# A fourth slab buffer, and the sums of weights in four pieces, in the gate and up stage of an encoder block

## The chip, the core and the metric

The kernel runs on one core of one Trainium2 chip. The metric is the time of one execution on the device in microseconds (us), the median of several runs. A core has a matrix engine (TensorE; PE in the profile, and PEld for its weight loads), three engines for elementwise work (VectorE or DVE, ScalarE or ACT, GpSimd or POOL), a queue engine (SyncE or SP) that issues most transfers here, and 16 DMA engines. Each engine has its own list of instructions and works it off in order; between engines, semaphores order them.

## What is computed

One encoder block on a sequence of 256 rows of width 2048: four mixers side by side, cross attention to a memory of 256 rows, and a gated feed forward part. Only the last bears on the change:

```
def swiglu(h, w_gate_up, w_down):
    gate, up = jnp.split(h @ w_gate_up, 2, axis=-1)
    return (jax.nn.silu(gate) * up) @ w_down
...
    x = x + swiglu(rms_norm(x, norm_g[l, 2]), w_gate_up[l], w_down[l])
```

`w_gate_up` is 2048 x 11264 and `w_down` 5632 x 2048, all in fp32.

## The kernel before

**Weights as one stream.** All weight matrices are cut into blocks of 128 x 128, in the order in which PE wants them. 16 blocks are a slab (128 x 2048, 1 MB in HBM, the rows `W[n]`), and there are 252 slabs. The class `Stream` loads and prepares them. One `dma_start` on SP's queue brings a slab into a tile `raw` (line 96), of which there are three (`rawp`, line 229). A slab is then split by halves of eight blocks: ACT rounds the half to the reduced format (`wh`, line 120), DVE forms what is left over (`wl`, line 121). A product is three matmuls: rounded left by rounded weight (line 421), by the leftover of the weight (422), and leftover of the left side by rounded weight (423). `wh` and `wl` have three buffers each (`wp`, line 230), and `look` (line 158) issues the split of a half when PE's work on the half two before is about to be issued. So a half's cast can begin when PE has left the half three before.

**Gate and up** (`gate_up`, line 855). The 11264 columns are taken in 11 groups `j` of 2 x 512 (512 of gate and the matching 512 of up). A group goes over the 16 row blocks of the contraction in eight slabs `i`, each with two of them (`2i` and `2i + 1`). An ordinary slab has four pieces of 128 x 512, each used by two halves of the rows: 8 x 3 = 24 matmuls of 128 x 512. The results of a group stay in four PSUM banks `cs`; odd groups have the banks `pm`, even groups `pg`.

**Summed slabs.** In each group but the first, the slabs `i` = 1 and 5 (`SEVEN`, line 47) are done as a 2 x 2 block product with seven products in place of eight, on sums of blocks of the left side and of the weight. That is 7 x 3 = 21 matmuls (`unit`, line 883). Of the slab's four pieces of 512 columns, three are used as they are (unsummed) and four sums are used: two differences to the first piece, and two further ones built on those. `Stream._forms` (line 125) makes them all when the slab's turn comes in `_half`: ACT rounds the unsummed 1536 columns (`hb`, line 134), DVE makes the sums `t` (lines 135 to 138), ACT rounds them (`ht`, lines 136 and 139), DVE forms the leftovers of the unsummed (`lb`, line 140) and of the sums (`lt`, line 142). These tiles have one buffer each. Lines 135, 138, 140 and 142 go through a helper, and the profile puts all of them at line 133: there the tiles' names `t`, `lb` and `lt` tell them apart. There are 20 such slabs. Their products go to four more PSUM banks (`ps`), which are those that the group before has left.

**What else DVE and ACT do there.** After slab 5 of a group `combine` (line 894) merges the four banks of the summed products: four operations on DVE (`m`, `h`, `g`, `h`), one copy on ACT (line 899). After slab 7 `finish` (line 908) adds two banks each for gate and up (four DVE operations at line 248), applies silu on ACT (line 915, `g<-g,rc`), multiplies (line 252, `h<-h,rc,g`), and turns the result (line 450, `u<-h`), which POOL's queue then stores (line 453, `hidden<-u`). `fetch` (line 839) reads the hidden rows of the first groups back while gate and up still runs and splits them (lines 256 and 248, `act<-tmp` and `f<-tmp`), and `turn` (line 972) turns the residual (line 979). The last two end before the middle of the stage.

**What sets the order.** This side work is written as generators in a list. `Background` (line 178) steps them between products: each step is due after some PE time, and only while the DVE work that is counted as owed (`dve`, line 196; it falls as PE's time goes on) is under 0.9 us. `drain` issues the rest of a generator at once: `finish` is drained when slab 1 of the next group comes. What is issued is then ordered by engine when the program is laid out: an instruction may be set before one that was issued earlier. `keep_place` (line 274) forbids that for chosen instructions: it ties each to the one issued before it on its engine.

The two lines that say when a split is issued, and how many halves ahead (`extra` is None in this stage):

```
ahead = self.n // 8 + 1 + min(3 if self.extra else 2, self.n // 16)
while len(self.halves) < min(ahead, NBLK // 8):
```

Of the kernel before, what the change touches and what calls it, by code (L numbers as in the profile page):

```python
# [13 lines left out]
F32 = mybir.dt.float32  # L14
F32R = mybir.dt.float32r
# [3 lines left out]
ALU = mybir.AluOpType  # L19
# [3 lines left out]
P = 128  # L23
# [11 lines left out]
CUTS = {0: [0, 256, 512, 1024, 2048]}  # L35
# [14 lines left out]
def seven(slab):  # L50

    j, i = divmod(slab - GU // 16, 8)
    return 1 <= j < DFF // 512 and i in SEVEN
# [22 lines left out]
class Stream:  # L76


    def __init__(self, tc, pools, W, bg):
        self.tc, self.nc, self.W, self.bg = tc, tc.nc, W, bg  # L80
        self.rawp, self.wp = pools
        self.order = []
        self.n = 0
        self.after = []
        self.halves = []
        self.raw = None
        self.extra = None
        self.places = []

    def _half(self):  # L90

        nc, n = self.nc, 8 * len(self.halves)
        if n % 16 == 0:
            self.raw = self.rawp.tile([P, 2048], F32, name="raw", tag="raw")
            for a, b in zip(CUTS[n], CUTS[n][1:]) if n in CUTS else [(0, 1024), (1024, 2048)] if self.after else [(0, 2048)]:
                (nc.scalar if (n, a) == (0, 0) else nc.sync).dma_start(self.raw[:, a:b], self.W[n // 16][:, a:b])
                if self.after:
                    self.after.pop(0)()
        if seven(n // 16):
            self.halves += [self._forms(self.raw), None]  # L100
            return
        o = (n % 16) * P
        r = self.raw[:, o:o + 1024]
# [12 lines left out]
        at = 48 if any(a <= n < b for a, b in ROWS) else 8  # L116
        wh, wl = wh[:, at:at + 1024], wl[:, at:at + 1024]
        edges = [0, 256, 512, 1024] if n == 0 else [0, 512, 1024] if n == 8 else [0, 1024]
        for a, b in zip(edges, edges[1:]):
            nc.scalar.copy(wh[:, a:b], r[:, a:b])  # L120
            nc.vector.tensor_tensor(out=wl[:, a:b], in0=r[:, a:b], in1=wh[:, a:b].bitcast(F32), op=ALU.subtract)  # L121
        self.bg.dve(1024)
        self.halves.append((wh, wl))

    def _forms(self, raw):


        nc = self.nc
        hb, lb, ht, lt = (self.swp.tile([P, w], F32R, name=t, tag=t)
                          for t, w in (("hb", 1536), ("lb", 1536), ("ht", 2048), ("lt", 2048)))  # L130
        t = self.swp.tile([P, 2048], F32, name="t", tag="t")
        blk = raw.rearrange("p (b c) -> p b c", b=4)
        sub = lambda out, a, b: nc.vector.tensor_tensor(out=out, in0=a, in1=b, op=ALU.subtract)  # L133
        nc.scalar.copy(hb, raw[:, 512:2048])  # L134
        sub(t[:, 0:1024].rearrange("p (b c) -> p b c", b=2), blk[:, 1:4:2, :], blk[:, 0:1, :].to_broadcast([P, 2, 512]))
        nc.scalar.copy(ht[:, 0:1024], t[:, 0:1024])
        nc.vector.tensor_tensor(out=t[:, 1024:1536], in0=raw[:, 1536:2048], in1=t[:, 0:512], op=ALU.add)
        sub(t[:, 1536:2048], raw[:, 1024:1536], t[:, 1024:1536])
        nc.scalar.copy(ht[:, 1024:2048], t[:, 1024:2048])
        sub(lb, raw[:, 512:2048], hb.bitcast(F32))  # L140
        for a in (0, 1024):
            sub(lt[:, a:a + 1024], t[:, a:a + 1024], ht[:, a:a + 1024].bitcast(F32))
        self.bg.dve(5632, 6)
        cut = lambda x, y: [(x[:, a:a + 512], y[:, a:a + 512]) for a in range(0, x.shape[1], 512)]
        return cut(hb, lb) + cut(ht, lt)

    def take_forms(self, w, ks, c0, c1):

        assert self.n % 16 == 0 and seven(self.n // 16)
        self.look()  # L150
        forms = self.halves[self.n // 8]
        for k, c in ((ks[0], c1), (ks[0], c0), (ks[1], c0), (ks[1], c1)):
            self.order += [(w, k, c + i * P) for i in range(4)]
        self.n += 16
        self.halves[self.n // 8 - 2] = None
        return forms

    def look(self):
        ahead = self.n // 8 + 1 + min(3 if self.extra else 2, self.n // 16)
# [60 lines left out]
class Block:  # L220
    def __init__(self, ctx, tc, t):
        self.ctx, self.tc, self.nc, self.t = ctx, tc, tc.nc, t
        pool = lambda n, b, **kw: ctx.enter_context(tc.tile_pool(name=n, bufs=b, **kw))
        self.cp = pool("cp", 1)
        self.tp = pool("tp", 11)
        self.rp = pool("rp", 3)
        self.psG = pool("psG", 4, space=PSUM)
        self.psM = pool("psM", 4, space=PSUM)
        rawp = pool("rawp", 3)
        wp = pool("wp", 3)  # L230
        self.bg = Background()
        self.st = Stream(tc, (rawp, wp), t["W"], self.bg)
        self.kept = itertools.count()
        self.run()

# [588 lines left out]
    def mlp(self):  # L824
        tc, nc, act = self.tc, self.nc, self.act
        with tc.tile_pool(name="fp", bufs=1) as fp:
            self.gap(fp, 192)
            f = act[4:12] + [fp.tile([P, 512], F32R, name=f"f{i}") for i in range(EARLY - 8)]
            with tc.tile_pool(name="sw", bufs=1) as sw, tc.tile_pool(name="gp", bufs=1) as gp:
                self.st.swp = sw  # L830
                self.gate_up(sw, gp, f)
            with tc.tile_pool(name="hp", bufs=1) as hp:
                held = [hp.tile([P, 512], F32R, name=f"held{i}") for i in range(HELD // 2)]
                self.st.places = list(zip(held[0::2], held[1::2]))
                f += [hp.tile([P, 512], F32R, name=f"g{i}") for i in range(FT - 16 - EARLY)] + self.h3
                self.bg.add(self.fetch(f, EARLY, FT, 6, SOON))
                self.down(f)
# [17 lines left out]
    def gate_up(self, sw, gp, f):  # L855

        nc, st = self.nc, self.st
# [24 lines left out]

        def unit(i, cs, ps, start, stop, c0, c1):

            b11, b21, b22, u1, t3, t2, t4 = st.take_forms("w_gate_up", (2 * i, 2 * i + 1), c0, c1)
            whole = lambda k, r: [self.h3[k][:, a + r * P:a + (r + 1) * P] for a in (0, R)]
            formed = lambda n: [x[:, n * P:(n + 1) * P] for x in sums[i]]
            for p, a, b, own in ((ps[0], whole(2 * i, 0), b11, True), (cs[0][0], whole(2 * i + 1, 0), b21, False),
                                 (cs[0][1], formed(3), b22, False), (ps[1], formed(0), u1, True), (ps[2], formed(2), t3, True),
                                 (ps[3], formed(1), t2, True), (cs[1][0], whole(2 * i + 1, 1), t4, False)):  # L890
                self.part(p, *a, *b, own and start, own and stop)
                self.bg.poll()

# [38 lines left out]
        forms = self.bg.add(left())  # L932
        turned = self.bg.add(self.turn())
        early = end = None
        for j in range(DFF // 512):
            cols = [j * 512, DFF + j * 512]
            banks = [self.gbank, self.bank]
            cs = [[banks[j % 2]() for _ in cols] for _ in range(2)]
# [4 lines left out]
            for i in range(8):  # L943
# [700 lines left out]
```

## Time and profile before

| | |
|---|---|
| median of 3 runs | 1485.53 us (1484.07, 1485.53, 1493.59) |
| the profiled execution | 1481.33 us, of which the span of instructions is 1479.6 us |
| granted TensorE clock | 0.998 of full speed |
| gate and up, groups 1 to 10 | from about 802 to 1222 us of the span |
| down, to the end | from about 1222 us |

How to read the profile: an engine's busy time is the union of its instructions. The ends of matmuls are modelled and a matmul's bar reaches over the start of the next, so that a stream of matmuls without gaps looks like PE busy all the time; the pace is read from start to start, or from the count of weight loads, of which there is one a matmul. "Idle before" is the time in which an engine stood idle ahead of an instruction, and after the arrow stands what ended it. A transfer's landing is counted from its issue.

### The profile page before, as it was taken

Reading aid. Unit: us, or ns where it says so; the run is one execution under the profiler, and the core shown is the slowest. Engines: PE = TensorE matmul, PEld = TensorE weight load, DVE = VectorE, ACT = ScalarE, POOL = GpSimd, SP = SyncE. Lnnn points to the kernel's source line nnn. Section 1 sums busy time; section 2 is a strip of 40 time slices with the busy share of each in tenths; the row PEclk is TensorE's granted clock in tenths of the full one; section 3 lists DMA queues with packets and bytes.
Section 4 is the critical chain, followed back from the end, with each engine's and each line's share of the span. In section 5 each row is a group of like instructions: output and inputs, shape, how many; then the busy total and the mean of one; then the engine's idle time right before and its main releaser. Section 6 shows DMA issues by size and latency. Waiting matters only on the chain.

```text
span 1479.6 us, 19468 instructions
## 1 busy us (share of the span) xinstructions
PE 1459.8 (99%) x7296; PEld 1230.8 (83%) x7296; DVE 1066.3 (72%) x1548; ACT 793.3 (54%) x1172; POOL 161.4 (11%) x276
## 2 busy tenths in 40 slices
PE   9999999999999999999999999999999999999997
PEld 7878888898898888888888787778888888888886
DVE  6688668778777767877776877878877776644445
ACT  6565655467555556766554454554454544534344
POOL 0220100000000001200024311111101112000000
PEclk9999999999999999999999999999999999999999
DMA  9975554454535555544557757656665675655554
GB/s 357 337 260 210 197 200 170 148 181 164 201 129 206 182 200 199 189 167 168 180 183 248 244 202 252 214 198 228 225 228 198 213 241 192 239 188 196 199 198 144
DMA packets 56718, 306.09 MB, mean 207 GB/s; under 512 B 9485, under 2 KB 11182, under 8 KB 25008
## 3 DMA queue, kind: packets, MB, share of 16 engines
q1 hardware_dynamic: 45920, 281.11, 53.5%
q0 software_dynamic: 10272, 23.09, 5.4%
q8 instruction: 57, 0.93, 0.2%
q10 hardware_dynamic: 432, 0.66, 0.1%
q14 instruction: 37, 0.30, 0.1%
HBM read 291.18 MB, written 13.63 MB: 206 GB/s over the span
## 4 chain that ended last, share of the span: by engine, by line
PE 75%; DVE 12%; DMA 8%; issue 3%; ACT 2%; SPq 0%; DVEq 0%; ACTq 0%
PE pg L370 18%; PE pg L422 11%; PE pg L423 11%; PE pg L421 11%; PE pg L371 10%; DMA raw<-in_W 8%; DVE wl L121 5%; PE pm L423 2%; PE pm L422 2%; PE pm L421 2%; DVE t L133 2%; DVE lt L133 2%; DVE lb L133 1%; PE pm L1145 1%; ACT wh L120 1%
## 5 line engine op out<-in xcount | busy, mean ns | idle before, releaser
L121 DVE TENSOR_TENSOR wl<-raw,wh 128x1024 fp32r<-128x1024 f32 (+1 forms) x463 | 559.4, 1214 | 269.2 <-ACT wh L120 264.1
L120 ACT CAST wh<-raw 128x1024 fp32r<-128x1024 f32 (+1 forms) x463 | 480.6, 1042 | 473.7 <-PE pg L423 219.8
L370 PE MATMUL pg<-act,wh 128*128 128x512 f32 x1104 | 389.2, 394 | 2.9 <-DVE act L248 2.9
L371 PE MATMUL pg<-act,wl 128*128 128x256 f32 x1216 | 341.4, 281 | 0.0
L422 PE MATMUL pg<-wl,act 128*128 128x512 f32 (+1 forms) x770 | 300.3, 390 | 4.4 <-DVE wl L121 4.3
L421 PE MATMUL pg<-wh,act 128*128 128x512 f32 (+1 forms) x770 | 300.8, 391 | 0.1
L423 PE MATMUL pg<-wh,act 128*128 128x512 f32 (+1 forms) x770 | 299.7, 389 | 0.0
L370 PEld LDWEIGHTS pg<-act,wh 128*128 128x128 f32 x1104 | 208.1, 189 | 48.5 <-DVE act L248 3.3
L371 PEld LDWEIGHTS pg<-act,wl 128*128 128x128 f32 x1216 | 229.2, 188 | 0.8 <-DVE wl L121 0.5
L422 PEld LDWEIGHTS pg<-wl,act 128*128 128x128 f32 x770 | 144.6, 188 | 38.0 <-DVE wl L121 8.3
L421 PEld LDWEIGHTS pg<-wh,act 128*128 128x128 f32 x770 | 144.5, 188 | 31.9 <-issue 1.2
L423 PEld LDWEIGHTS pg<-wh,act 128*128 128x128 f32 x770 | 144.5, 188 | 29.9
L422 PE MATMUL pm<-wl,act 128*128 128x512 f32 x272 | 106.6, 392 | 2.8 <-DVE wl L121 2.7
L423 PE MATMUL pm<-wh,act 128*128 128x512 f32 x272 | 105.9, 389 | 0.0
L421 PE MATMUL pm<-wh,act 128*128 128x512 f32 x272 | 105.9, 389 | 0.0
L453 POOL DMA_DIRECT2D hidden<-u x88 | 56.8, 653 | 320.0 <-DVE u L450 317.9
L133 DVE TENSOR_TENSOR t<-raw 128x1024 f32<-128x1024 f32 x20 | 24.5, 1225 | 58.7 <-DMA raw<-in_W 58.7
L422 PEld LDWEIGHTS pm<-wl,act 128*128 128x128 f32 x272 | 51.1, 188 | 15.8 <-DVE wl L121 5.2
L134 ACT CAST hb<-raw 128x1536 fp32r<-128x1536 f32 x20 | 29.6, 1480 | 60.4 <-DMA raw<-in_W 55.3
L421 PEld LDWEIGHTS pm<-wh,act 128*128 128x128 f32 x272 | 51.1, 188 | 10.7
L423 PEld LDWEIGHTS pm<-wh,act 128*128 128x128 f32 x272 | 51.1, 188 | 10.3
L133 DVE TENSOR_TENSOR lt<-t,ht 128x1024 fp32r<-128x1024 f32 x40 | 48.0, 1216 | 0.0
(386 smaller groups left out, 1864.8 us busy)
## 6 DMA issues: line engine op xcount, KB each, us to landing
raw<-in_W SPq DMA_DIRECT2D x246, 1024.0 KB, 5.0
raw<-in_W SPq DMA_DIRECT2D x11, 512.0 KB, 7.6
hidden<-u POOLq DMA_DIRECT2D x88, 64.0 KB, 4.5
tmp<-hidden POOLq DMA_DIRECT2D x44, 128.0 KB, 4.7
res<-in_xT SPq DMA_DIRECT2D x8, 512.0 KB, 6.1
k<-in_mem SPq DMA_DIRECT2D x8, 256.0 KB, 7.7
k<-in_x SPq DMA_DIRECT2D x8, 256.0 KB, 8.6
keys<-k POOLq DMA_DIRECT2D x32, 64.0 KB, 5.2
```

Of the source, the lines that this page charges most:

```text
L120: nc.scalar.copy(wh[:, a:b], r[:, a:b])
L121: nc.vector.tensor_tensor(out=wl[:, a:b], in0=r[:, a:b], in1=wh[:, a:b].bitcast(F32), op=ALU.subtract)
L133: sub = lambda out, a, b: nc.vector.tensor_tensor(out=out, in0=a, in1=b, op=ALU.subtract)
L134: nc.scalar.copy(hb, raw[:, 512:2048])
L370: self.nc.tensor.matmul(p[:, :], wh, slot[:, :], start=start, stop=False)
L371: self.nc.tensor.matmul(p[:, 0:R], wl, slot[:, 0:R], start=False, stop=stop)
L421: self.nc.tensor.matmul(p, hi, wh, start=start, stop=False)
L422: self.nc.tensor.matmul(p, hi, wl, start=False, stop=False)
L423: self.nc.tensor.matmul(p, lo, wh, start=False, stop=stop)
L453: nc.gpsimd.dma_start(to[:, :, 32 * a:32 * a + 32], u[32 * a:32 * a + 32, :].rearrange("f (b t) -> f b t", t=32))
L1145: self.b.nc.tensor.matmul(p, a, b, start=start and n == 0, stop=stop and n == 2)
```

## The change

- `raw(slab)` takes the loads out of `_half`. While gate and up runs, every fourth slab (those whose number leaves 3 when divided by 4) has its tile in a pool of its own, `rawx`; the others keep the three of `rawp`. The tiles `hb` and `lb` (12 KB a partition together) go, `rawx` (8 KB) comes.
- `_forms` becomes `_sums(slab, part)`. Parts 0 and 1 are issued with the first and second half of the slab before the summed one (so the summed slab's load is issued there too), part 2 with the summed slab's first half. Each is tied to its place by `keep_place`, and each counts its own DVE time.
- The unsummed 1536 columns are split in `_half` like all others: 512 columns with the summed slab's first half, 1024 with the second, into `wh` and `wl`.
- `take_forms` becomes a generator: it hands out the seven pairs of weights one by one, and calls `look` a second time, after the first product. `unit` walks it beside the list of its products.

```
+    def raw(self, slab):
+        while len(self.raws) <= slab:
+            n = 16 * len(self.raws)
+            pool = self.rawx if self.rawx and len(self.raws) % 4 == 3 else self.rawp
+            self.raws.append(pool.tile([P, 2048], F32, name="raw", tag="raw"))
...
+        return self.raws[slab]
+
     def _half(self):
-        nc, n = self.nc, 8 * len(self.halves)
-        if n % 16 == 0:
-            self.raw = self.rawp.tile([P, 2048], F32, name="raw", tag="raw")
...
-        if seven(n // 16):
-            self.halves += [self._forms(self.raw), None]
-            return
+        nc, h = self.nc, len(self.halves)
+        n = 8 * h
+        if seven(h // 2 + 1):
+            self._sums(h // 2 + 1, h % 2)
+        elif seven(h // 2) and h % 2 == 0:
+            self._sums(h // 2, 2)
+        raw = self.raw(n // 16)
...
-        edges = [0, 256, 512, 1024] if n == 0 else [0, 512, 1024] if n == 8 else [0, 1024]
+        edges = [0, 256, 512, 1024] if n == 0 else [0, 512, 1024] if n == 8 else [512, 1024] if seven(h // 2) and h % 2 == 0 else [0, 1024]
...
-    def _forms(self, raw):
...
+    def _sums(self, slab, part):
+        nc, raw = self.nc, self.raw(slab)
+        if part == 0:
+            self.forms = [self.swp.tile([P, 2048], dt, name=t, tag=t) for t, dt in (("t", F32), ("ht", F32R), ("lt", F32R))]
+        t, ht, lt = self.forms
+        mark = len(nc.cur_bb.bb.instructions)
+        op = lambda out, a, b, what=ALU.subtract: nc.vector.tensor_tensor(out=out, in0=a, in1=b, op=what)
+        low = lambda a: op(lt[:, a:a + 1024], t[:, a:a + 1024], ht[:, a:a + 1024].bitcast(F32))
+        if part == 0:
+            blk = raw.rearrange("p (b c) -> p b c", b=4)
+            op(t[:, 0:1024].rearrange("p (b c) -> p b c", b=2), blk[:, 1:4:2, :], blk[:, 0:1, :].to_broadcast([P, 2, 512]))
+            nc.scalar.copy(ht[:, 0:1024], t[:, 0:1024])
+            self.bg.dve(1024)
+        elif part == 1:
+            op(t[:, 1024:1536], raw[:, 1536:2048], t[:, 0:512], ALU.add)
+            op(t[:, 1536:2048], raw[:, 1024:1536], t[:, 1024:1536])
+            nc.scalar.copy(ht[:, 1024:2048], t[:, 1024:2048])
+            low(0)
+            self.bg.dve(2048, 3)
+        else:
+            low(1024)
+            self.bg.dve(1024)
+        self.keep(mark)
...
     def take_forms(self, w, ks, c0, c1):
         assert self.n % 16 == 0 and seven(self.n // 16)
         self.look()
-        forms = self.halves[self.n // 8]
         for k, c in ((ks[0], c1), (ks[0], c0), (ks[1], c0), (ks[1], c1)):
             self.order += [(w, k, c + i * P) for i in range(4)]
-        self.n += 16
-        self.halves[self.n // 8 - 2] = None
-        return forms
+        cut = lambda x, y, a: (x[:, a:a + 512], y[:, a:a + 512])
+        yield cut(*self.halves[self.n // 8], 512)
+        self.n += 8
+        self.look()
+        for a in (0, 512):
+            yield cut(*self.halves[self.n // 8], a)
+        for a in (0, 512, 1024, 1536):
+            yield cut(*self.forms[1:], a)
+        self.n += 8
+        self.halves[self.n // 8 - 1] = self.halves[self.n // 8 - 2] = None
...
-            with tc.tile_pool(name="sw", bufs=1) as sw, tc.tile_pool(name="gp", bufs=1) as gp:
+            with tc.tile_pool(name="sw", bufs=1) as sw, tc.tile_pool(name="rawx", bufs=1) as self.st.rawx, tc.tile_pool(name="gp", bufs=1) as gp:
                 self.st.swp = sw
                 self.gate_up(sw, gp, f)
+            self.st.rawx = None
```

More of the change, by code (lines that the diff above doesn't have):

```diff
@@ L85, in __init__, with _half @@
         self.halves = []
-        self.raw = None
-        self.extra = None
+        self.raws = []
+        self.rawx = self.extra = None
         self.places = []
-    def _half(self):
-        nc, n = self.nc, 8 * len(self.halves)
-        if n % 16 == 0:
-            self.raw = self.rawp.tile([P, 2048], F32, name="raw", tag="raw")
+    def raw(self, slab):
[3 more added lines that the diff above has]
+            self.raws.append(pool.tile([P, 2048], F32, name="raw", tag="raw"))
             for a, b in zip(CUTS[n], CUTS[n][1:]) if n in CUTS else [(0, 1024), (1024, 2048)] if self.after else [(0, 2048)]:
-                (nc.scalar if (n, a) == (0, 0) else nc.sync).dma_start(self.raw[:, a:b], self.W[n // 16][:, a:b])
+                (self.nc.scalar if (n, a) == (0, 0) else self.nc.sync).dma_start(self.raws[-1][:, a:b], self.W[n // 16][:, a:b])
                 if self.after:
                     self.after.pop(0)()
-        if seven(n // 16):
-            self.halves += [self._forms(self.raw), None]
-            return
+        return self.raws[slab]
+    def _half(self):
+        nc, h = self.nc, len(self.halves)
[5 more added lines that the diff above has]
+        raw = self.raw(n // 16)
         o = (n % 16) * P
-        r = self.raw[:, o:o + 1024]
+        r = raw[:, o:o + 1024]
         if n >= NBLK - HELD:
@@ L123, in _half @@
         self.halves.append((wh, wl))
-    def _forms(self, raw):
[L128 to L145, printed above, removed]
@@ L232, in __init__ @@
         self.st = Stream(tc, (rawp, wp), t["W"], self.bg)
+        self.st.keep = self.keep_place
         self.kept = itertools.count()
@@ L883, in unit @@
         def unit(i, cs, ps, start, stop, c0, c1):
-            b11, b21, b22, u1, t3, t2, t4 = st.take_forms("w_gate_up", (2 * i, 2 * i + 1), c0, c1)
             whole = lambda k, r: [self.h3[k][:, a + r * P:a + (r + 1) * P] for a in (0, R)]
             formed = lambda n: [x[:, n * P:(n + 1) * P] for x in sums[i]]
-            for p, a, b, own in ((ps[0], whole(2 * i, 0), b11, True), (cs[0][0], whole(2 * i + 1, 0), b21, False),
-                                 (cs[0][1], formed(3), b22, False), (ps[1], formed(0), u1, True), (ps[2], formed(2), t3, True),
-                                 (ps[3], formed(1), t2, True), (cs[1][0], whole(2 * i + 1, 1), t4, False)):
+            for (p, a, own), b in zip(((ps[0], whole(2 * i, 0), True), (cs[0][0], whole(2 * i + 1, 0), False),
+                                       (cs[0][1], formed(3), False), (ps[1], formed(0), True), (ps[2], formed(2), True),
+                                       (ps[3], formed(1), True), (cs[1][0], whole(2 * i + 1, 1), False)),
+                                      st.take_forms("w_gate_up", (2 * i, 2 * i + 1), c0, c1), strict=True):
                 self.part(p, *a, *b, own and start, own and stop)
```

## The prediction

> **What bounds the kernel now.** The page comes first, for what the core is made of.
>
> ```profile
> span 1479.6 us, 19468 instructions
> PE 1459.8 (99%) x7296; PEld 1230.8 (83%) x7296; DVE 1066.3 (72%) x1548; ACT 793.3 (54%) x1172; POOL 161.4 (11%) x276
> raw<-in_W SPq DMA_DIRECT2D x246, 1024.0 KB, 5.0
> ```
>
> PE is busy in all but 1479.6 - 1459.8 = 19.8 us, and the change leaves out no matmul: a summed slab has seven parts of three matmuls before and after. So all that it can win is PE time lost in gate and up. To size that I read the windows view (columns: busy us and count of PE, PEld, DVE, ACT, POOL, then clock, DMA share, GB/s): a pair of slab groups without a gap, then gate and up from column group 1 on, whole and in two stretches.
>
> ```profile
> 1024.91:1067.07 42.16, 42.16 (x187) 34.91 (x186) 34.27 (x37) 20.97 (x21) 7.39 (x12) 1.00 0.66 236
> 802.00:1222.00 420.00, 415.36 (x1819) 340.49 (x1820) 338.13 (x373) 208.03 (x223) 76.94 (x125) 1.00 0.64 221
> 802.00:984.00 182.00, 177.76 (x773) 144.36 (x774) 147.54 (x171) 92.63 (x107) 39.90 (x66) 1.00 0.65 225
> 984.00:1222.00 238.00, 237.61 (x1047) 196.13 (x1047) 190.59 (x203) 115.40 (x117) 37.04 (x59) 1.00 0.63 219
> ```
>
> In the first row PE never idles, and 186 weight loads, one a matmul, take 42.16 us: 0.2267 us each. At that pace the 1820 of the whole stage take 412.5 of its 420.0 us: **7.5 us are lost**. The stretch to 984 loses 182.0 - 774 x 0.2267 = 6.6 us, the rest 0.7 us. This is more than the idle time in the rows (4.6 us), because the matmul after a gap is slow too. Which wait it is stands in the waits view of PE (us in total, times, longest), and one gap in PE's timeline:
>
> ```profile
> PE pg L422 <- DVE wl L121: 4.3, 7, 1.5
> PE pm L422 <- DVE wl L121: 2.7, 4, 1.1
> 867.18 0.39 PE L421 MATMUL pg<-wh,act 128*128 128x512 f32 x1
> 867.91 0.50 PE L422 MATMUL pg<-wl,act 128*128 128x512 f32 x1 [0.35 <-DVE wl L121]
> 868.25 0.39 PE L423 MATMUL pg<-wh,act 128*128 128x512 f32 x1
> ```
>
> PE waits for the low part wl of an ordinary half slab. The next matmul starts 0.34 us after the late one, not 0.23. Then the DVE's timeline ahead of that gap, and the chain of waits there:
>
> ```profile
> 854.96 2.35 DVE L121 TENSOR_TENSOR wl<-raw,wh 128x1024 fp32r<-128x1024 f32 x2
> 862.09 1.23 DVE L133 TENSOR_TENSOR t<-raw 128x1024 f32<-128x1024 f32 x1 [4.79 <-DMA raw<-in_W]
> 863.23 1.22 DVE L121 TENSOR_TENSOR wl<-raw,wh 128x1024 fp32r<-128x1024 f32 x1
> 864.37 0.68 DVE L137 TENSOR_TENSOR t<-raw,t 128x512 f32<-128x512 f32 x1
> 864.97 1.75 DVE L133 TENSOR_TENSOR lb<-raw,hb 128x1536 fp32r<-128x1536 f32 x1
> 866.64 1.22 DVE L121 TENSOR_TENSOR wl<-raw,wh 128x1024 fp32r<-128x1024 f32 x1
> ...
> 859.21 1.05 ACT L120 CAST wh<-raw 128x1024 fp32r<-128x1024 f32 x1 [5.44 <-PE pg L423]
> ...
> 853.93 2.25 DVE wl L121 x2
> 856.20 5.87 DMA raw<-in_W
> 862.09 1.23 DVE t L133
> ```
>
> This is the whole mechanism. A load of a slab starts when the last wl of three slabs before has freed its buffer (856.20), lands 5.87 us later, and DVE, in order, stands idle for 4.79 us at the first sum t. Behind t stands a wl whose cast was done at 859.21 + 1.05 = 860.26, and behind lb another, which ends at 867.86 when PE wanted it at 867.41. (The order on an engine is not the code's: the code writes lb after the sums, the row has it between them.) Over the stage this head of line is paid 19 times:
>
> ```profile
> DVE t L133 <- DMA raw<-in_W: 56.3, 19, 5.2
> SPq L96 <- DVE wl L121: 366.5, 63, 11.9
> L96 SPq DMA_DIRECT2D raw<-in_W x89: 327/328/1003, 764.3 to 1237.7; - x89
> DMA to landing us min/median/max: 4.8/6.2/8.9
> ```
>
> **The change part by part.** Durations of the operations it touches, by shape (count | busy us, mean ns):
>
> ```profile
> L121 DVE TENSOR_TENSOR wl<-raw,wh 128x1024 fp32r<-128x1024 f32 x119 | 142.4, 1214 | 14.8 <-ACT wh L120 14.7
> L133 DVE TENSOR_TENSOR lt<-t,ht 128x1024 fp32r<-128x1024 f32 x40 | 48.0, 1216 | 0.0
> L133 DVE TENSOR_TENSOR lb<-raw,hb 128x1536 fp32r<-128x1536 f32 x19 | 33.3, 1752 | 0.3 <-ACT hb L134 0.3
> L133 DVE TENSOR_TENSOR t<-raw,t 128x512 f32<-128x512 f32 x20 | 13.7, 683 | 0.0
> L134 ACT CAST hb<-raw 128x1536 fp32r<-128x1536 f32 x20 | 29.6, 1480 | 60.4 <-DMA raw<-in_W 55.3 <-PE pm L423 5.1
> L264 ACT CAST w3h<-k 128x512 fp32r<-128x512 f32 x18 | 11.2, 622 | 5.5 <-PE pm L1145 3.0 <-DVE k L248 2.3
> L120 ACT CAST wh<-raw 128x1024 fp32r<-128x1024 f32 x458 | 478.1, 1047 | 471.2 <-PE pg L423 219.8 <-PE pg L370 84.0 <-PE pm L423 57.2
> ```
>
> (1) *Fourth slab buffer.* A load now waits for the last wl of four slabs before, so it starts one slab earlier: an ordinary slab is 24 matmuls, 24 x 0.2267 = 5.44 us. The load of the rows above would land at 856.65 instead of 862.09, while DVE is still in the pair of wl that ends at 857.31. Even the longest landing (8.9 us, 3.0 over the 5.87 here) leaves 2.4 us. The loads are the same 1 MB each and the DMA share is 0.64, so nothing is added there; SP issues the same list of loads in the same order, 0.33 us each (the row x89 above), and the summed slab's is moved past no other; POOL's queue keeps its list too.
>
> (2) *Sums in four pieces, two of them a slab ahead.* Pieces: t for the two differences with its cast, with the splits of the first half of the slab before; the other two t with their cast and the first lt, with its second half; the second lt with the summed slab's own first half. The fourth piece is the blocks' split. The same DVE work is spread over three half slabs (1.22; 0.68 + 0.68 + 1.22 = 2.58; 1.22 us) in place of one lump ahead of ordinary wl's. Each piece is pinned behind the DVE or ACT instruction issued before it, so t cannot stand ahead of an older wl any more. Behind a piece is one wl with its cast: that split may begin when PE leaves the half three before, and has 2 x 2.72 us. Cast 1.05 and wl 1.21 leave 3.2 us, of which the largest piece takes 2.58, and part of it runs before that buffer is free. Cost on the path: nothing; cover gone (DVE late already) up to the 0.7 to 1.3 us that such a piece exceeds a half's slack in a stretch with other DVE work.
>
> (3) *Unsummed blocks split like all others.* Per summed slab DVE gives lb (1.75) for a 512 wide wl (taken as the 512 wide t, 0.68) and a 1024 wide one (1.21): +0.15 us. ACT gives hb (1.48) for 0.62 + 1.05: +0.19 us. Twenty slabs: 3.0 us of DVE and 3.8 us of ACT, in a stage where they are busy 338 and 208 of 420 us; on the path zero. The Trainium skill (Perfetto Trace Analysis, Optimizing Scalar/DVE Operations) speaks against this cut: larger operations help if the engine is saturated. By that rule 3.0 us would be added to the time; but the same section says that smaller pieces may finish sooner where DVE is not saturated and makes bubbles elsewhere, and at 81% busy with 56.3 us spent waiting for loads the trace is in that second case.
>
> (4) *A new wait.* The unsummed blocks had a buffer of their own, free for three slabs. Now they turn with the other halves through three buffers. For the summed slab's second half the cast may start when PE leaves the first half of the slab before, 2.72 us before the summed slab, and PE wants wl one part and one matmul in (4 x 0.2267 = 0.91 us): 3.63 us for 1.05 + 1.21, a slack of 1.37 us, twenty times. Where that slab starts a column group, DVE also has to finish the group before. How that looks now:
>
> ```profile
> 1062.27 1.22 DVE L133 TENSOR_TENSOR lt<-t,ht 128x1024 fp32r<-128x1024 f32 x1
> 1063.40 1.28 DVE L248 TENSOR_TENSOR g<-pg,g 128x512 f32<-128x512 f32 x2
> 1064.60 1.28 DVE L248 TENSOR_TENSOR h<-pg,h 128x512 f32<-128x512 f32 x2
> 1065.80 1.40 DVE L252 SCALAR_TENSOR_TENSOR h<-h,rc,g 128x512 f32<-128x512 f32 x2
> 1067.12 1.29 DVE L450 STREAM_TRANSPOSE u<-h 128x512 f32<-128x512 f32 x2
> 1068.34 3.45 DVE L121 TENSOR_TENSOR wl<-raw,wh 128x1024 fp32r<-128x1024 f32 x3
> 1064.12 1.34 ACT L915 ACTIVATE g<-g,rc 128x512 f32<-128x512 f32 x2 [0.68 <-DVE g L248]
> ```
>
> Eight operations take 1063.40 to 1068.34, 4.9 us in a row, and wl's queue behind. If only the two first adds (1.28) stand ahead of the new wl, it is in time; if all eight do, it is late: they can start when the slab's first half is split, 0.62 + 0.68 = 1.3 us after the group's start, end at 6.2, and wl at 7.4, against 5.44 + 0.91 = 6.35 when PE wants it: 1.05 us. Ends: 0 and 10 groups x 1.05 = 10.5 us. No gain can come of a wait that is added. The four adds are what the code issues by the middle of that slab at most, so I take nearer to zero: 1.0 us in all.
>
> *Sum.* Won: the 7.5 us; kept back 0.6 for gaps where the reads of early hidden rows and the turned residual fall together before 984 us; lost 1.0. Net 5.9 us. The profiled execution took 1481.33 us (span 1479.6 and 1.7 around it): 1475.4. It lies 4.2 us under the median of the runs shown, 1485.53 (1484.07 to 1493.59); against that median the forecast is **1479.6 us**.
>
> **The rivals.** *Slower: finish ahead of the new split.* Place: the second half of the first summed slab of each group; price 1.05 us by the worked case, ten times, 10.5 us against 7.5 won: 1488.5. It decides from 0.75 us each. For it: the eight in a row above. Against it: they are issued one by one as the count of owed DVE time falls, most after that split. Chance 0.14.
>
> *The waits stay, only their cause moves.* After 984 us t waits as long as before (a share of the 56.3), yet PE loses only 0.7 us: the wait alone makes no gap, it takes the extra splits and turns of the first groups. If it is these that make wl late, perhaps a third goes: 1483.0. Against it: each summed slab wins 56.3 / 19 = 3.0 us of DVE time, twice the longest gap (1.5). Chance 0.2.
>
> *The change does not do what it says*: loads start no earlier because something else than the buffer holds SP. SP's 366.5 us of waiting for wl, 63 times in 89 loads, speaks against: 1485.5 at 0.06.
>
> **How the numbers follow.** Forecast 0.6 (1476 to 1482), waits stay 0.2, no change 0.06, slower by finish 0.14. Nothing in the stage can be won beyond 7.5 us, 0.5%; with half of the 4.2 us between profile and median as noise the low end is 1475.5. The high end takes in the slower case: 1488.5. About 1% is what a measurement of this kernel can tell from no change, 14.9 us here: faster than that is out of reach (0.01), slower needs the 10.5 us with nothing won and more beside it, or a cause not listed (0.04), so 0.95 within.
>
> **What would show it.** Right: t no longer waits for raw (56.3 us to under 10), the load's issue lies a slab earlier, 420 us of this stage become about 414, DVE busy rises by some 3 us, PE waits for wl at L121's successor under 1.5 us. Wrong: PE waits of the second unsummed half beside the finish operations; ordinary wl late behind a sum piece although raw had landed; or t still idle behind raw.

## The result, and the profile after

| | before | after |
|---|---|---|
| median | 1484.07 us (7 runs, 1481.18 to 1493.59) | 1472.38 us (7 runs, 1470.38 to 1474.71) |
| ratio | | 0.9915, 95% interval 0.989 to 0.994 |
| profiled execution | 1481.33 us, span 1479.6 | 1473.38 us, span 1471.6 |

The kernel became faster by 0.6 to 1.1%. The forecast was 1479.6 us, and the range began at 1475.5: the time lies below it.

First the changed kernel's page: span, engines, and the chain of work that ended last.

```profile
span 1471.6 us, 19530 instructions
PE 1456.4 (99%) x7296; PEld 1232.5 (84%) x7296; DVE 1072.1 (73%) x1568; ACT 799.6 (54%) x1192; POOL 161.9 (11%) x276
PE 98%; DVE 1%; ACT 1%; DMA 0%; issue 0%; SPq 0%; DVEq 0%; ACTq 0%
```

The same line of the chain in the page of the kernel before:

```profile
PE 75%; DVE 12%; DMA 8%; issue 3%; ACT 2%; SPq 0%; DVEq 0%; ACTq 0%
```

PE is 99% busy in both pages; the chain is what tells them apart. Before, 22% of it ran over DVE, the loads and ACT, and 3% were issue. Now it is PE's own.

The windows view of the changed kernel, over the stretches used in the prediction:

```profile
802.00:1222.00 420.00, 420.00 (x1855) 347.89 (x1853) 345.65 (x394) 216.36 (x245) 77.18 (x125) 1.00 0.66 221
802.00:984.00 182.00, 182.00 (x805) 150.75 (x803) 153.10 (x183) 97.45 (x117) 45.22 (x74) 1.00 0.68 231
984.00:1222.00 238.00, 238.00 (x1052) 197.14 (x1050) 192.55 (x211) 118.90 (x129) 31.96 (x51) 1.00 0.64 214
```

1853 weight loads x 0.22667 us are 420.0 us: nothing is lost in this window, where the profile of before lost 7.5. That is nearly the whole difference between the two profiles (1479.6 - 1471.6 = 8.0 us of span).

The waits view of the changed kernel, 795 to 1230 us:

```profile
ACT wh L129 <- PE pg L443: 99.8, 51, 4.4
ACT wh L129 <- PE pm L443: 89.3, 45, 4.4
DVE wl L130 <- ACT wh L129: 74.2, 49, 4.0
```

And the landing of its loads, from the view by tile:

```profile
DMA to landing us min/median/max: 4.8/5.0/7.5
```

No row of t waiting for raw is left (it was 56.3 us, 19 times), and no row of PE waiting. What ACT waits for is PE, which frees its buffers, and DVE's wl waits for ACT: so a bound by PE looks from the other engines here. In the kernel before, PE's waits from 802 to 1222 us were these two rows:

```profile
PE pm L422 <- DVE wl L121: 2.7, 4, 1.1
PE pg L422 <- DVE wl L121: 2.1, 4, 1.0
```

The prediction's rows, seven and four waits, are of the whole execution: three of them, the longest of 1.5 us among them, lie in its first 80 us, and the changed kernel has three there too (1.9 us, the longest 1.5).

The DVE timeline at the place that the prediction showed (the second summed slab of group 2):

```profile
857.90 1.22 DVE L130 TENSOR_TENSOR wl<-raw,wh 128x1024 fp32r<-128x1024 f32 x1 [2.32 <-ACT wh L129]
859.04 0.42 DVE L268 TENSOR_TENSOR act<-tmp,act 128x256 fp32r<-128x256 f32 x1
859.38 1.22 DVE L142 TENSOR_TENSOR t<-raw 128x1024 f32<-128x1024 f32 x1
860.61 1.23 DVE L130 TENSOR_TENSOR wl<-raw,wh 128x1024 fp32r<-128x1024 f32 x1
861.75 0.42 DVE L268 TENSOR_TENSOR act<-tmp,act 128x256 fp32r<-128x256 f32 x1
862.09 1.41 DVE L142 TENSOR_TENSOR t<-raw,t 128x512 f32<-128x512 f32 x2
863.42 1.22 DVE L142 TENSOR_TENSOR lt<-t,ht 128x1024 fp32r<-128x1024 f32 x1
864.55 1.22 DVE L130 TENSOR_TENSOR wl<-raw,wh 128x1024 fp32r<-128x1024 f32 x1
865.69 1.22 DVE L142 TENSOR_TENSOR lt<-t,ht 128x1024 fp32r<-128x1024 f32 x1
866.83 0.69 DVE L130 TENSOR_TENSOR wl<-raw,wh 128x512 fp32r<-128x512 f32 x1
```

The three pieces of the sums stand where the code puts them (one t; the other two t and an lt; the second lt), each with one wl behind it, and t starts without a gap.

### The profile page after: what moved, and what is told of

It reads as the page before. It is cut to its first block, busy times and chain, and to the rows that moved or that the text cites. A ratio compares the mean times of both kernels' runs of the same rounds, so it can differ in the third digit from the quotient of the medians.

```text
span 1471.6 us, 19530 instructions
## 1 busy us (share of the span) xinstructions
PE 1456.4 (99%) x7296; PEld 1232.5 (84%) x7296; DVE 1072.1 (73%) x1568; ACT 799.6 (54%) x1192; POOL 161.9 (11%) x276
## 4 chain that ended last, share of the span: by engine, by line
PE 98%; DVE 1%; ACT 1%; DMA 0%; issue 0%; SPq 0%; DVEq 0%; ACTq 0%
PE pg L390 18%; PE pg L442 15%; PE pg L441 15%; PE pg L443 15%; PE pg L391 10%; PE pm L443 6%; PE pm L441 6%; PE pm L442 6%; PE pm L1166 1%; PE pg L387 1%; PE pg L388 1%; PE pm L837 1%; PE pm L810 1%; DMA raw<-in_W 0%; DVE wl L130 0%; PE pm L1546 0%
## 5 line engine op out<-in xcount | busy, mean ns | idle before, releaser
L130 DVE TENSOR_TENSOR wl<-raw,wh 128x1024 fp32r<-128x1024 f32 (+1 forms) x503 | 597.5, 1194 | 324.3 <-ACT wh L129 318.5
L129 ACT CAST wh<-raw 128x1024 fp32r<-128x1024 f32 (+1 forms) x503 | 513.9, 1027 | 540.8 <-PE pg L443 267.5
L441 PE MATMUL pg<-wh,act 128*128 128x512 f32 (+1 forms) x790 | 308.7, 391 | 0.8 <-ACT wh L129 0.8
L442 PE MATMUL pg<-wl,act 128*128 128x512 f32 (+1 forms) x790 | 307.4, 389 | 1.9 <-DVE wl L130 1.9
L443 PE MATMUL pg<-wh,act 128*128 128x512 f32 (+1 forms) x790 | 307.4, 389 | 0.0
L441 PEld LDWEIGHTS pg<-wh,act 128*128 128x128 f32 x790 | 148.5, 188 | 33.2 <-ACT wh L129 1.2
L443 PEld LDWEIGHTS pg<-wh,act 128*128 128x128 f32 x790 | 148.4, 188 | 31.0
L441 PE MATMUL pm<-wh,act 128*128 128x512 f32 x292 | 113.6, 389 | 0.0
L442 PE MATMUL pm<-wl,act 128*128 128x512 f32 x292 | 113.6, 389 | 0.0
L443 PE MATMUL pm<-wh,act 128*128 128x512 f32 x292 | 113.6, 389 | 0.0
L441 PEld LDWEIGHTS pm<-wh,act 128*128 128x128 f32 x292 | 54.8, 188 | 11.4
L442 PEld LDWEIGHTS pm<-wl,act 128*128 128x128 f32 x292 | 54.8, 188 | 11.4
L443 PEld LDWEIGHTS pm<-wh,act 128*128 128x128 f32 x292 | 54.8, 188 | 11.3
L1003 POOL DMA_DIRECT2D xrows<-tmp x48 | 27.8, 586 | 140.1 <-DVE rc L268 123.7
L268 DVE TENSOR_TENSOR tmp<-pg,tmp 128x256 f32<-128x256 f32 x78 | 32.4, 418 | 5.2 <-ACT tmp L397 4.4
```

What stands on the lines that cost most here:

```text
L268: self.nc.vector.tensor_tensor(out=out, in0=a, in1=b, op=op)
L441: self.nc.tensor.matmul(p, hi, wh, start=start, stop=False)
L442: self.nc.tensor.matmul(p, hi, wl, start=False, stop=False)
L443: self.nc.tensor.matmul(p, lo, wh, start=False, stop=stop)
L1003: nc.gpsimd.dma_start(to[:, :, c:c + 32], u[32 * a:32 * a + 32, :].rearrange("t (b f) -> t b f", f=32))
```

## The experiments

There are fifteen runs: three repeat a kernel as it is, twelve are of edited kernels. They were taken in four rounds, each beside the kernel before, whose median was 1481.92, 1482.95, 1481.66 and 1482.10 us in them; each ratio is to the kernel before of its own round. For each profile one number is worked out in the same way: the PE time lost between 802 and 1222 us, 420.0 us less the count of weight loads x 0.22667. It is called *lost* below; a count can be off by three, 0.7 us.

**1. Where do executions of one kernel differ?** The profile of before took 1481.33 us, its timed runs 1481.18 to 1493.59, and the changed kernel gained 11.7 us on the median, more than the 7.5 that the profile had lost. So the kernel before was profiled twice more, and the changed one once, without an edit.

> The kernel before, unchanged, profiled once more. Theory 1 (the time lost in gate and up hangs on how fast each slab lands, so it differs from execution to execution): time minus the PE time lost between the first and the last summed slab is the same as in the first profile, 1481.3 - 7.5 = 1473.8 us, within 1 us; an execution at 1485 us shows some 11 us lost. Theory 2 (executions differ elsewhere, in the clock or ahead of the stage): the stage loses 7.5 us again whatever the time, and the difference stands before 760 or after 1225 us.

> The same once more, for a third point. Theory 1: time minus lost time is 1473.8 us within 1 us. Theory 2: lost time is 7.5 us within 1 us.

> The changed kernel, unchanged, profiled once more. Both theories: 0 to 0.5 us lost in the stage; time 1470 to 1475 us. Were the lost time here above 1 us, the stage would still depend on the landing of loads.

The stage's windows row of before_again1:

```profile
802.00:1222.00 420.00, 414.64 (x1818) 339.93 (x1817) 338.32 (x373) 208.20 (x224) 76.95 (x125) 1.00 0.64 221
```

Of before_again2:

```profile
802.00:1222.00 420.00, 413.06 (x1804) 336.99 (x1803) 335.74 (x369) 208.02 (x223) 76.93 (x125) 1.00 0.64 220
```

Of after_again:

```profile
802.00:1222.00 420.00, 420.00 (x1855) 347.96 (x1854) 345.60 (x393) 216.07 (x245) 76.94 (x125) 1.00 0.67 221
```

| profile | time | lost | time less lost |
|---|---|---|---|
| before, first | 1481.33 | 7.5 | 1473.8 |
| before_again1 | 1482.17 | 8.1 | 1474.1 |
| before_again2 | 1485.71 | 11.3 | 1474.4 |
| after | 1473.38 | 0.0 | 1473.4 |
| after_again | 1472.41 | 0.0 | 1472.4 |

Theory 1 holds: what differs from execution to execution is the loss in this stage, and what is left is the same in both kernels within 2 us. The window can be checked, since the 7296 matmuls stand in the same order in every trace. From the first matmul of group 1 to the first behind group 10 there are 1860, 421.6 us at the pace. The three profiles of before take 429.8, 430.1 and 433.0 us for them, both of the changed kernel 421.6. So the loss is 8.2, 8.5 and 11.4 us; the window ends too early for the kernel before, whose stage ends at 1231 us in its first profile and not at 1222. Ahead of the stage the five profiles differ by less than 2 us, behind it by less than 0.1.

The loss goes with the waits for loads (t idle for 56.3, 58.6 and 62.4 us in these three profiles). The kernel that waits for loads spreads over 12 us from the lowest to the highest of its seven runs, the changed kernel over 4. The run before_tied below loses 10.9 us without a wait of t for its load, and its twelve executions lie within 4 us too. That it is the landings which differ from run to run rests on these few profiles.

**2. Is it the side work that makes t's wait a loss?** The kernel before, with both pieces of side work moved:

```
-        turned = self.bg.add(self.turn())
...
-                early = self.bg.add(self.fetch(f, 0, EARLY, 3, 2.0))
+            if j == 6:
+                turned = self.bg.add(self.turn())
+                early = self.bg.add(self.fetch(f, 0, EARLY, 3, 2.0))
```

> The kernel before, with the reading back of hidden rows and the turning of the residual started in group 6 instead of groups 1 and 0; the work is the same. If the wait of the first sum for its load makes PE wait by itself, the lost time stays spread as before, most of it in groups 1 to 4 (6.6 of 7.5 us). If it takes this side work on the vector engine as well (the prediction's second rival in its mild form), groups 1 to 4 lose under 1.5 us and groups 6 to 9 lose 4 to 8 us; the total time is within 0.3% of before either way.

1477.15 us, ratio 0.9976 (0.996 to 0.9992). The two stretches in its windows view:

```profile
802.00:984.00 182.00, 180.50 (x792) 148.11 (x791) 144.90 (x158) 86.74 (x88) 44.46 (x73) 1.00 0.67 225
984.00:1222.00 238.00, 236.63 (x1041) 194.85 (x1041) 194.52 (x219) 119.40 (x132) 50.99 (x85) 1.00 0.66 227
```

Lost: 182.0 - 791 x 0.22667 = 2.7 us (6.6 before) and 238.0 - 1041 x 0.22667 = 2.0 us (0.7 before). Both expectations missed. The side work makes more of the waits late for PE: the first stretch lost 6.6, 5.9 and 7.2 us in the three profiles of before. But with none beside them the first groups still lose 2.7 us. The 2.0 us of the second stretch tell nothing, since the profiles of before lost 0.7, 2.0 and 3.8 us there without side work (the last is 238.0 - 1033 x 0.22667).

**3. Which part of the change does it?** First, parts taken out of the changed kernel. Three buffers:

```
-            pool = self.rawx if self.rawx and len(self.raws) % 4 == 3 else self.rawp
+            pool = self.rawp
```

> The changed kernel with three slab buffers instead of four; pieces, places and the split of the unsummed blocks stay. Theory A (the load's start is what counts): a load waits again for the slab three before, so it lands about where the first piece is now due, a slab earlier than the lump was; t still idles behind raw, 30 us or more in all over the stage, and PE loses 4 us or more, ratio to before 0.995 or higher. Theory B (the place counts: pinned, t can no longer stand ahead of an older wl, and what idles has no wl behind it that is due): t may idle, yet PE loses under 1.5 us, ratio 0.992.

All the sums in one lump at the summed slab's first half, tied to no place (`self.st.keep = lambda mark: None`), with four buffers:

```
-        if seven(h // 2 + 1):
-            self._sums(h // 2 + 1, h % 2)
-        elif seven(h // 2) and h % 2 == 0:
-            self._sums(h // 2, 2)
+        if seven(h // 2) and h % 2 == 0:
+            for part in range(3):
+                self._sums(h // 2, part)
```

> The changed kernel with its four buffers and its split of the unsummed blocks, but all the sums issued in one lump at the summed slab's own first half, tied to no place, as before. Theory A: loads start a slab earlier, t idles under 10 us, PE loses under 1.5 us, ratio 0.992. Theory B: the lump still stands ahead of wl's that are due, 5 us of vector work at once against a slack of 3.2 us, and PE loses 4 us or more, ratio 0.995 or higher.

Both edits at once, so that of the change only the split of the unsummed blocks is left (and the second `look` that comes with it):

> Only the split of the unsummed blocks changed against the kernel before: three buffers, sums in one lump, tied to no place. Prediction's parts 3 and 4 alone: 3 us more vector work and the new wait of the summed slab's second half, 0 to 10.5 us on the path. Theories A and B both: t idles 50 to 65 us, ratio 1.000 to 1.003. If the new wait costs nothing in this layout, 1.000 within its interval.

And the change whole, but with no instruction tied to its place:

```
-        self.st.keep = self.keep_place
+        self.st.keep = lambda mark: None
```

> The changed kernel whole, but its pieces are not tied to their places. Theory A: no difference to the changed kernel, PE loses under 0.5 us, ratio 0.992. Theory B: pieces stand ahead of older wl's again; with four buffers their loads have mostly landed, so PE loses 1 to 4 us, ratio 0.993 to 0.995.

Then the kernel before with single parts added. The second `look` alone:

```
-        self.n += 16
-        self.halves[self.n // 8 - 2] = None
-        return forms
+        yield forms[0]
+        self.n += 8
+        self.look()
+        yield from forms[1:]
+        self.n += 8
+        self.halves[self.n // 8 - 2] = None
...
```

> The kernel before, with one thing of the change: the summed slab's weights are handed out one by one, and the splits ahead are looked after once more after its first product (so that the second half of the next slab, and the load behind it, are issued half a slab earlier). Unsummed blocks keep their own tiles. Theory C (two thirds of the gain, which the split of the unsummed blocks brought along with it, are this second look): ratio 0.995 to 0.996, t idles about 30 us. Theory D (they come of the lump that is shorter by the leftovers of the unsummed blocks, 1.75 us of the vector engine and 1.48 us of casting, and of the order that follows): ratio 0.999 to 1.001, t idles 50 to 65 us.

The split of the unsummed blocks without it (three_buffers_lump with that `self.look()` taken out):

> The other half: unsummed blocks split like all others, three buffers, one lump, and the splits ahead looked after only once in the summed slab. Theory C: ratio 0.999 to 1.001. Theory D: 0.995 to 0.996, t idles about 30 us.

The fourth buffer alone, its room made by `EARLY = 12` (four blocks of hidden rows less are read back early), and the control with that line alone:

```
-EARLY = 16
+EARLY = 12
...
-            self.raw = self.rawp.tile([P, 2048], F32, name="raw", tag="raw")
+            pool = self.rawx if self.rawx and n // 16 % 4 == 3 else self.rawp
+            self.raw = pool.tile([P, 2048], F32, name="raw", tag="raw")
...
```

> The kernel before with the fourth slab buffer and nothing else of the change. To make room for it, 12 instead of 16 blocks of hidden rows are read back while gate and up runs, four less in the first groups. If the load's start is the cause (theory A), t idles under 10 us, PE loses under 1 us, ratio 0.992 to 0.993. If the lump of 6.8 us with its casts stays in the way of older wl's although the slab has landed, PE loses 2 to 4 us, ratio 0.994 to 0.996.

> The control to the one above: the kernel before with 12 instead of 16 blocks read back early, three buffers. Expected ratio 0.998 to 1.000 (four splits of 0.8 us each less beside the first groups); what lies below that in the run with the fourth buffer is the buffer's.

And the kernel before with its lump tied to the place where the code issues it (`keep_place` over `_forms`):

> The kernel before, with its lump of sums tied to the place at which the code issues it, behind all older wl's; three buffers, unsummed blocks in their own tiles. If the split of the unsummed blocks helped by the order alone (t no longer ahead of wl's that are due), this helps as much: t idles under 30 us, ratio 0.995 to 0.996. If it helped because the lump is 1.75 us shorter, tying gives nothing or harms, because the whole lump then comes late for its own products: ratio 0.999 to 1.005, PE waits for lb or lt.

| kernel | median us | ratio to before, 95% interval | lost | t idle for raw, 802 to 1222 |
|---|---|---|---|---|
| before | | 1 | 7.5, 8.1, 11.3 | 56.3, 58.6, 62.4 |
| three_buffers | 1475.54 | 0.9949 (0.9935 to 0.9963) | 4.5 | 22.1 |
| four_buffers_lump | 1472.59 | 0.9924 (0.9912 to 0.9937) | 0 | 4.7 |
| three_buffers_lump | 1475.28 | 0.9948 (0.9934 to 0.9963) | 3.6 | 26.6 |
| not_tied | 1471.99 | 0.9924 (0.9911 to 0.9936) | 0 | 5.3 |
| second_look_only | 1480.15 | 0.9987 (0.9971 to 1.0004) | 5.2 | 51.9 |
| split_one_look | 1476.22 | 0.9961 (0.9947 to 0.9974) | 2.9 | 25.1 |
| fourth_buffer_only | 1474.45 | 0.9949 (0.9933 to 0.9965) | 0 | 2.7 |
| less_read_back | 1481.12 | 0.9998 (0.9984 to 1.0013) | 8.6 | 60.8 |
| before_tied | 1481.80 | 0.9993 (0.9979 to 1.0007) | 10.9 | none |

The stage's windows row and t's wait on which this rests, of fourth_buffer_only:

```profile
802.00:1222.00 420.00, 420.00 (x1855) 347.77 (x1854) 340.61 (x367) 214.33 (x219) 74.91 (x121) 1.00 0.65 220
DVE t L134 <- DMA raw<-in_W: 2.7, 3, 1.7
```

Of three_buffers:

```profile
802.00:1222.00 420.00, 417.31 (x1834) 343.16 (x1833) 346.03 (x393) 215.65 (x244) 76.94 (x125) 1.00 0.67 221
```

- *The fourth buffer alone takes the whole loss away*, with the lump, the tiles of the unsummed blocks and the code's order of the kernel before. Theory A holds for PE's loss; t's idle time without the buffer (22.1 us in three_buffers) is less than the 30 it named. The ratio of fourth_buffer_only missed the 0.992 to 0.993 that was expected and lies where the other theory had it; but that theory's loss in the stage is not there. Its time is higher than the changed kernel's by a wait behind the stage, which the room for the buffer costs; PE's waits from 1230 to 1300 us in it:

```profile
PE pg L422 <- ACT g L257: 1.4, 1, 1.4
```

  And in the control, less_read_back:

```profile
PE pg L421 <- ACT g L256: 1.4, 1, 1.4
```

  A hidden row that is read back later comes late once. The changed kernel has no such wait. From the first matmul behind group 10 to the last of all, both kernels with this wait take 2.1 us more than all five profiles of experiment 1 (242.1 and 242.2 beside 240.0 us): without them, 1474.45 us would be about the changed kernel's 1472.4.
- *With four buffers, neither the pieces a slab ahead nor the ties add anything*: lump, untied pieces and the changed kernel all lose nothing. Nor does the place count that the layout finds for the first t: it starts 19.0 us ahead of PE's first matmul on the slab in fourth_buffer_only, 15.7 in four_buffers_lump and 12.0 in the changed kernel (12.8 in the kernel before; medians of the 20).
- *With three buffers, the split of the unsummed blocks alone takes more than half of the loss away.* This was not expected by theory A or B. It is not the second `look` (theory C; its ratio can't be told from 1, and t idles 51.9 us), so theory D is left, which named a shorter lump and the order that follows. The pieces on top of it add nothing that can be measured (0.9949 beside 0.9948).
- *The order alone is not it.* Tied behind the older wl's, t waits for raw no more (one wait of 1.4 us in all, ahead of 802 us), and PE loses 10.9 us all the same. PE's waits in before_tied, 795 to 1230 us:

```profile
PE pg L425 <- DVE wl L121: 2.5, 5, 0.5
PE pm L425 <- DVE wl L121: 2.2, 4, 0.8
PE pg L425 <- DVE lb L134: 1.5, 2, 1.3
PE pm L425 <- DVE lb L134: 1.2, 1, 1.2
```

  The summed slabs' loads had landed by then, so three buffers are early enough for a lump at this place (ACT's casts still waited for other loads, 11.2 us in ten waits); but there the lump is late for its own products (lb) and for the wl's behind it. Where the layout had set it, earlier, it waits for raw: neither of the two places tried is good with three buffers and the whole lump. What in the split of the unsummed blocks eases this with three buffers (a lump shorter by lb's 1.75 us, or another place that the layout finds for it) is left open: the runs do not separate these. An earlier load it is not. In three_buffers_lump the load of a summed slab is issued 16.9 us ahead of PE's first matmul on that slab (median of the 20), in the kernel before 18.3 us.
- *What the buffer does to the loads.* By the same measure it is 21.2 us in the changed kernel and 26.5 us in fourth_buffer_only. The summed slabs' loads also land faster in the changed kernel, in 5.0 us against 5.6 (medians). Of the two, the earlier issue (2.9 us) is the larger part.

**4. How much room does DVE have?** In the changed kernel, the first `low(0)` of part 1 is done twice, or four times, into the same place.

```
-            low(0)
-            self.bg.dve(2048, 3)
+            low(0)
+            low(0)
+            self.bg.dve(3072, 4)
```

> The changed kernel with the first leftover of the sums formed twice in each of the 20 summed slabs: 20 x 1.2 = 24 us more vector work, nothing else. Theory (vector engine is busy 346 of 420 us and no longer waits for loads, so what is added in a slab ahead is hidden): under 1 us of PE waits, time within 1 us of the changed kernel's 1472.4. Rival (it is at its limit around the group's end, where the operations of finish stand): PE loses 3 us or more, in the groups' first slabs.

> The same with three more: 72 us more vector work, 418 of 420 us busy. Theory: now the vector engine is the bound in the stage; PE loses 5 to 40 us, waiting for wl. Were nothing lost, the place of the pieces would hide far more than the busy time says.

The stage's windows row with one more piece:

```profile
802.00:1222.00 420.00, 419.97 (x1849) 346.23 (x1849) 366.90 (x411) 215.32 (x244) 76.94 (x125) 1.00 0.66 222
```

With three more:

```profile
802.00:1222.00 420.00, 403.00 (x1733) 322.12 (x1732) 384.95 (x415) 198.20 (x216) 71.08 (x115) 1.00 0.61 205
```

Some 24 us more DVE work (busy 367 of 420 us, 346 in the changed kernel) lose 420.0 - 1849 x 0.22667 = 0.9 us, little more than the count can be off; the median is 1473.78 us, 1.4 us above the changed kernel's where 1 us at most was expected, and of its ratio, 0.9935 (0.9914 to 0.9956), the interval takes in the changed kernel's 0.9915. With 72 us more, 27.4 us are lost, within the 5 to 40 that were expected, and the kernel is slower than before: 1501.09 us, 1.0129 (1.0102 to 1.0155). DVE is then busy for 385 us and not for 418, as the window holds fewer products. The room ends between the two.

## Why the prediction was wrong

**What bounds the kernel: right.** 7.5 us lost, by wl's behind a t that waits for its load. The changed kernel loses none of it, and the two profiles differ by 8.0 us of span. One reading was wrong and changed no term of the sum: the longest gap in the stage was 1.1 us and not 1.5, as said above.

**The step that failed is the last of the sum:** "It lies 4.2 us under the median of the runs shown, 1485.53 ... against that median the forecast is 1479.6 us". That took the 4.2 us between the profile and the median for something that both kernels have. Where executions of the kernel before were longer, they had lost more in the stage: time less lost is 1473.8 to 1474.4 us in three profiles of before, and 1472.4 to 1473.4 in two of the changed kernel. The median itself was that of three executions, and a high one: in the four later rounds it was 1481.7 to 1483.0 us, so that the profile stood for a usual execution. The sum should have been taken to where the loss ends, 1481.33 - 7.5 = 1473.8 us, with nothing added: 1.4 us from the median measured. With the 4.2 us and the 1.6 of the next paragraph these are the 7.2 us by which the forecast missed. For the same reason "Nothing in the stage can be won beyond 7.5 us" held for that one execution only, and the low end of the range with it; another lost 11.3 us. (The low end is also not what its own terms give: 1485.53 - 7.5 - 2.1 is 1475.9 and not 1475.5.)

**Terms of the sum.** Kept back 0.6 us for gaps beside the side work, measured none. For the new wait (part 4) 1.0 us, measured none: PE has no wait in the stage. Both made the forecast higher by 1.6 us.

**Part 1, the fourth buffer: right, and it is all of the loss.** Alone it brings the loss to zero. Its size was only roughly right: a slab, 5.44 us, was taken, and against PE's first matmul on the slab the load is issued 2.9 us earlier for the summed slabs and 4.7 us for the others (21.2 us ahead, 16.5 before; medians).

**Part 2, the pieces: at the right price, zero, but with a share in the argument that they do not have.** They are not needed beside the buffer, and without it they leave 4.5 us of loss, where the split alone leaves 2.9 and 3.6.

**Part 3, the split of the unsummed blocks: the price was right and a gain was missed.** The 512 wide wl takes 683 ns, as taken. On the path it costs nothing. The rule of the Trainium skill weighed there (Perfetto Trace Analysis, Optimizing Scalar/DVE Operations: larger operations help a saturated engine) would have added 3.0 us. The runs put the stage in the other case: even 24 us more cost 0.9. That it takes half of the loss away with three buffers, the prediction did not see: it bounded the cost from below by zero ("on the path zero"). It also makes the room for the buffer, as `hb` and `lb` go.

**The rivals.** Finish ahead of the new split cost nothing: PE has no wait in the stage. "The waits stay, only their cause moves" had a true half: the side work does make the first groups' waits worse (6.6 to 2.7 us without it), but they need the load's wait: with the fourth buffer and all but four of the read-backs in their place (fourth_buffer_only), nothing is lost. "Does not do what it says" fell: t's waits are gone.

**What would show it.** t's wait for raw under 10 us (none), the stage's work in 420 us (now without loss), DVE more by some 3 us for the same work: it is 345.7 against 338.1 us in the window, but the window now holds 1853 instead of 1820 matmuls, and 338.13 x 1853 / 1820 = 344.3, so by this estimate 1.4 us are more. The load's issue lies 2.9 us earlier for the summed slabs, not a slab.

## What to carry to other kernels

A kernel whose busiest engine waits a little for loads can have a time that differs from run to run, as here; a forecast for a change that removes the waits goes to the floor, the profile's time less what it lost, and not to a median of a few runs less that loss. When an in-order engine stands idle at the head of its queue, look first at when the transfer behind it could have started: here one more buffer made the order of the work behind it indifferent. Take the parts of a change one by one on the chip even when the whole has gained, since here one of three took the whole loss away, another served to make its room, and the third added nothing.

## What the runs showed of the hardware beside that

The same 1 MB loads land faster in the changed kernel: median 6.2 us before, 5.0 after (760 to 1240 us), at a DMA share of 0.64 and 0.66 in the stage. It is not the number of buffers, since before_tied, with three, has 5.2; what it is was not tried.

A wait of PE costs more than the idle time that its row shows. In the gap of the prediction the row has 0.35 us. But the late matmul starts 0.73 us after the one before it, and its successor 0.34 us later, where the pace is 0.23: 0.50 and 0.11 us more, 0.6 us in all. So the eight waits of the first profile, 4.8 us of idle time, stand for 6.9 of the 7.5 us lost. The prediction put the difference down to the slow successors alone.
